# First norm's sums taken from a token-major copy of x on ScalarE; the low halves of w_in kept in DRAM after the first block

## Chip, core and metric

One core of a Trainium2 chip runs the whole layer in one launch. The metric is device time in microseconds (us) of that core. Five engines each work through their own list of instructions in order: PE (TensorE), DVE (VectorE), ACT (ScalarE), POOL (GpSimd) and SP (SyncE), which here issues every DMA. An instruction that must wait holds up all that stands behind it on its engine.

## The reference, cut to what matters

The layer works on 2048 tokens of 1024 channels in float32. What the change touches is the first norm and the first projection:

```
def rms_norm(x, g):
    ms = jnp.mean(x * x, axis=-1, keepdims=True)
    return x * lax.rsqrt(ms + EPS) * g

h = rms_norm(x, norm1_g)        # (2048, 1024)
proj = h @ w_in                 # (1024, 1536): 512 columns u, 512 xr, 512 yr
s5_out  = s5_mixer(proj[:, :512], ...)            # diagonal state space scan, GELU, GLU
lru_out = rglru_mixer(proj[:, 512:1024], proj[:, 1024:], ...)  # conv(4), gates, scan
mix = concat(rms_norm(s5_out), rms_norm(lru_out))
x = x + mix @ w_out
x = x + (silu(h2 @ w_gate) * (h2 @ w_up)) @ w_down,  h2 = rms_norm(x, norm2_g)
return rms_norm(x, final_g)
```

## The kernel before, in words

**Layout.** x lies in DRAM transposed (`xT`: channels by tokens), so a tile is 128 channels by 512 tokens. The 2048 tokens form four blocks of 512. Each float32 product is made of three matmuls in a faster float format: an operand a is split into a high half (`hi`, the value cast to that format) and a low half (`lo`, the value minus `hi`), and a·b is taken as hi·hi + hi·lo + lo·hi (`mm3`, L198).

**Input projection, `in_tb(b, t0)`, once for each block.** It splits x into `actH` and `actL` (L276 on ACT, L277 on DVE) and then runs 12 units, one for each 128 columns of `w_in`. A unit has two weight tiles ("parts") of 128x512, so a block has 24 parts. Class `Unit` loads a part (`wraw`, six buffers, L181), casts it on ACT (`whi`, four buffers, L187) and subtracts (`wlo`, four buffers, L188): on DVE for two units of three, on POOL for the third. The same parts of `w_in` are loaded and split again in each of the four blocks. The results are scaled by the norm's factor `rs` when they leave PSUM: `conv` (L627), `evac_u` (L618) and `gate_y` (L682), all on DVE. The first four units go through `conv` and `gates`, then come the gated recurrence (`decay`, `scan`) and `lru_out`.

**The norm's factor.** `SumSq` squares the eight channel tiles of a block on ACT (L238) and adds them up tile by tile on POOL (L240). In block 0 half of the squares are on POOL (L236) and the adds on DVE. `finish` sums over partitions with four small matmuls (L246), takes the reciprocal root in some twelve small DVE instructions (`rsqrt`, L210 to L218, tile `nv`), and spreads the result over partitions with four more matmuls (L256) and an ACT copy into `rs` (L259). In blocks 1 to 3 the tiles are loaded a second time for it, well ahead, through one buffer (`xq`, L272): a load waits until ACT has squared the tile before it.

**The S5 branch** runs beside the blocks. `s5_build` computes its tables on DVE, starting after the first `rsqrt`; POOL and PE help, and the tables go to DRAM (`md`). Its eight slices for the first half of the tokens (`s5_in`, `s5_scan`, `s5_out`) run during blocks 2 and 3 and end in `zb`, which the stage after the projection reads. After the four blocks come GLU and output projection (`glu_tb`, `out_tb`), then the feed-forward network with its weights split in the same way (L995, L996, matmuls L1156 and L1296).

**What sets the order.** The code files each step under a planned time (`at(t, fn)`) and emits the steps in order of these times; a scheduler with a timeline model of its own then sets the order of each engine's list. All DMAs stand in SP's one list. A DMA that writes a tile waits there until the tile's last reader is done, and each DMA also waits for the one eight before it.

Of the kernel before, what the change touches and what calls it, by code (L numbers as in the profile page):

```python
# [9 lines left out]
F32 = mybir.dt.float32  # L10
# [12 lines left out]
CT = 8  # L23
# [56 lines left out]
def build(tc, nc, I, O, ctx):  # L80
# [49 lines left out]
    td = dram("td", (2, 7, NSL, 128, TB))  # L130
    rld = dram("rld", (NB, TB))
# [36 lines left out]
    class Unit:  # L168


        def __init__(self, t, src, nk, eng=None):
            eng = DV if eng is None else eng
            self.parts = []
            for i in range(0, nk, 4):
# [8 lines left out]
                def split(part=part, n=n):  # L183
                    raw = part.pop("raw")[:, :n, :]
                    hi = part["hi"] = P.tile([128, 4, 128], R, tag="whi", name="whi", bufs=4)
                    lo = part["lo"] = P.tile([128, 4, 128], R, tag="wlo", name="wlo", bufs=4)
                    AC.copy(hi[:, :n, :], raw)  # L187
                    eng.tensor_tensor(out=lo[:, :n, :], in0=raw, in1=hi[:, :n, :].bitcast(F32), op=ALU.subtract)  # L188

                at(t + i * PT - 18.0, load)  # L190
                at(t + i * PT - 6.0, split)
# [30 lines left out]
    class SumSq:  # L222


        def __init__(self, n, tag="sum", bufs=1, room=(), dv=False):
            self.n, self.i, self.s, self.tag, self.bufs, self.room, self.dv = n, 0, None, tag, bufs, room, dv

        def add(self, ap):
            i, n = self.i, self.n
            self.i += 1  # L230
            if i == 0:
                q = self.s = A.tile([128, TB], F32, tag=self.tag, name=self.tag, bufs=self.bufs)
            else:
                q = self.room[i - 1] if i <= len(self.room) else t2("sq")
            if self.room and i % 2 == 0:
                GP.tensor_tensor(out=q, in0=ap, in1=ap, op=ALU.mult)  # L236
            else:
                AC.activation(out=q, in_=ap, func=AF.Square)  # L238
            if i:
                (DV if self.room or self.dv else GP).tensor_tensor(out=self.s, in0=self.s, in1=q, op=ALU.add)  # L240

        def finish(self, dst=None):
# [4 lines left out]
            y = rsqrt(ps[:, 0:4], 128 * self.n)  # L247
            ps = aux("nm")
# [344 lines left out]
    def in_tb(b, t0):  # L593
        H, L = actH, actL
        cur = {}
        room = [t[:, i, :] for t in xrp for i in range(2)] if b == 0 else ()
        ss, sl = SumSq(8, room=room), SumSq(4, "sumg", 2)
        tx, dx = (t0 - 6.5, 0.5) if b == 0 else (t0 - 5.0, 0.6)
        for k in range(8):
# [10 lines left out]
            if b == 0:  # L610
                at(tx + k * dx + 1.5, lambda k=k: ss.add(cur["x", k]))
            else:
                at(t0 - 62 + 1.5 * k, lambda k=k: ss.add(load_chunk(xT, b, k, pL, "xq", 1)))
        at(t0 + 0.1 if b == 0 else t0 - 48, lambda: cur.__setitem__("rs", ss.finish()))
# [884 lines left out]
```

## Time and profile before

| | us |
|---|---|
| median of 3 runs (lowest, highest) | 2208.16 (2206.6, 2210.63) |
| the profiled execution | 2207.93 |
| its span, first to last instruction | 2206.2 |
| four input blocks | 0 to 495 |
| GLU and output projection | 495 to 825 |
| feed-forward | 825 to 2206 |

The bounds of the stages are read from PE's rows of L198 and L1156: the first matmul of a block's 288 stands at 7, 122, 252 and 374 us, the last one of block 3 ends at 495. The page's times are in us from the first instruction. A group's row gives the line, the engine, the operation, output and inputs by the program's names, how often, and behind the bar the busy time, the mean in ns, and the idle time of the engine just before with what ended it. A row of a stretch (0.00:122.00) gives its length and, for each engine, the busy time and the number of instructions, then the granted PE clock as a share of full speed, the share of time in which the 16 DMA engines were busy, and GB/s.

### The profile page before, as it was taken

To read this page: it belongs to the slowest core of one execution; us is meant where nothing else is said; L and a number is where in the kernel's file an instruction comes from. 1 tells how busy PE (TensorE), PEld (TensorE's weight loads), DVE (VectorE), ACT (ScalarE), POOL (GpSimd) and SP (SyncE) were. 2 spreads that over 40 slices of the span, in tenths; PEclk is the share of its full clock that TensorE was granted. 3 is DMA by queue.
4 is the path that set the end of the run, shared out by engine and by line. 5 is a ranking of instruction groups with operands and counts; after the bars stand their busy time and mean duration, and the time that the engine had idled before them with its cause. 6 is when DMAs were issued, how large, how long until landed. Compare 5 with 4: busy or idle time off the path is not lost.

```text
span 2206.2 us, 26290 instructions
## 1 busy us (share of the span) xinstructions
PE 1988.3 (90%) x8632; PEld 1582.2 (72%) x8632; DVE 1335.3 (61%) x1975; ACT 812.1 (37%) x1336; POOL 1114.2 (51%) x904
## 2 busy tenths in 40 slices
PE   7668888878988978799999989999999999999996
PEld 5546666656766856577777767777777788888885
DVE  9998868759957397444444474444444535554744
ACT  4433644364344333223233253233232333333331
POOL 3768556649755377654554561231322326644442
PEclk9868999989898988899999999999999999999998
DMA  6244795573763687744444474443443568854733
GB/s 203 86 130 135 196 224 163 180 174 122 234 203 110 206 276 243 257 154 151 149 155 142 151 254 138 134 148 125 145 137 125 171 214 316 301 163 144 247 101 100
DMA packets 251754, 386.37 MB, mean 175 GB/s; under 512 B 59328, under 2 KB 81120, under 8 KB 251616
## 3 DMA queue, kind: packets, MB, share of 16 engines
q1 hardware_dynamic: 251616, 384.69, 55.5%
q8 instruction: 68, 1.11, 0.2%
q14 instruction: 70, 0.57, 0.1%
HBM read 267.92 MB, written 116.67 MB: 174 GB/s over the span
## 4 chain that ended last, share of the span: by engine, by line
PE 63%; DVE 16%; DMA 8%; POOL 5%; issue 4%; ACT 2%; SPq 1%; POOLq 0%; DVEq 0%; ACTq 0%
PE acc L1156 9%; PE gt L1156 9%; PE y L1156 9%; PE acc L198 6%; PE y L1296 5%; PE v L1156 5%; PE acc L1296 5%; PE gt L1296 5%; PE nm L1156 4%; PE nm L1296 2%; PE v L1296 2%; DVE wlo L188 2%; POOL s_s L824 2%; DMA xq<-xT 2%; DVE xh L633 1%
## 5 line engine op out<-in xcount | busy, mean ns | idle before, releaser
L1169 POOL TENSOR_TENSOR t<-t 128x512 f32<-128x512 f32 x66 | 100.6, 1525 | 343.8 <-DVE t L1195 242.2
L198 PE MATMUL acc<-actH,whi 128*128 128x512 f32 x528 | 219.5, 418 | 55.6 <-DVE gy L682 14.0
L995 ACT CAST whi<-ws 128x512 fp32r<-128x512 f32 x176 | 109.1, 620 | 343.1 <-PE gt L1156 91.8
L198 PE MATMUL acc<-actL,whi 128*128 128x512 f32 x528 | 219.7, 417 | 12.9 <-DVE actL L277 12.9
L198 PE MATMUL acc<-actH,wlo 128*128 128x512 f32 x528 | 217.5, 412 | 0.0
L996 DVE TENSOR_TENSOR wlo<-ws,whi 128x512 fp32r<-128x512 f32 x176 | 145.1, 825 | 67.3 <-ACT whi L995 65.3
L996 DVE TENSOR_TENSOR wlo<-ht,whi 128x512 fp32r<-128x512 f32 x112 | 106.0, 949 | 120.6 <-ACT whi L995 120.5
L198 PEld LDWEIGHTS acc<-actH,whi 128*128 128x128 f32 x528 | 105.7, 200 | 87.2 <-issue 35.1
L995 ACT CAST whi<-ht 128x512 fp32r<-128x512 f32 x154 | 95.0, 618 | 168.9 <-PE nm L1296 73.4
L1156 PE MATMUL y<-xh,whi 128*128 128x512 f32 x308 | 124.8, 405 | 16.9 <-ACT t L1188 12.0
L187 ACT CAST whi<-wraw 128x512 fp32r<-128x512 f32 x176 | 106.1, 613 | 86.5 <-PE acc L198 66.2
L996 POOL TENSOR_TENSOR wlo<-ht,whi 128x512 fp32r<-128x512 f32 x42 | 56.7, 1349 | 160.4 <-ACT whi L995 160.3
L198 PEld LDWEIGHTS acc<-actL,whi 128*128 128x128 f32 x528 | 105.6, 200 | 40.9 <-DVE actL L277 19.3
L1156 PE MATMUL acc<-xh,wlo 128*128 128x512 f32 x308 | 124.0, 403 | 8.4 <-DVE wlo L996 8.4
L1156 PE MATMUL acc<-xh,whi 128*128 128x512 f32 x308 | 124.6, 404 | 4.3 <-ACT xh L995 2.3
L1156 PE MATMUL y<-xh,wlo 128*128 128x512 f32 x308 | 123.4, 401 | 5.1 <-DVE wlo L996 5.1
L1156 PE MATMUL y<-xl,whi 128*128 128x512 f32 x308 | 123.9, 402 | 3.7 <-DVE xl L996 3.7
L188 POOL TENSOR_TENSOR wlo<-wraw,whi 128x512 fp32r<-128x512 f32 x64 | 93.9, 1470 | 64.2 <-ACT whi L187 63.7
L188 DVE TENSOR_TENSOR wlo<-wraw,whi 128x512 fp32r<-128x512 f32 x112 | 101.9, 914 | 39.1 <-ACT whi L187 32.3
L1156 PE MATMUL acc<-xl,whi 128*128 128x512 f32 x308 | 123.7, 402 | 1.4 <-DVE xl L996 1.4
L198 PEld LDWEIGHTS acc<-actH,wlo 128*128 128x128 f32 x528 | 106.3, 201 | 23.3 <-issue 0.9
L1156 PE MATMUL gt<-xh,whi 128*128 128x512 f32 x308 | 122.2, 397 | 0.5 <-DVE t L1193 0.5
(421 smaller groups left out, 5522.0 us busy)
## 6 DMA issues: line engine op xcount, KB each, us to landing
td<-t SPq DMA_DIRECT2D x154, 256.0 KB, 2.2
ht<-td SPq DMA_DIRECT2D x154, 256.0 KB, 2.8
wraw<-w_down SPq DMA_DIRECT2D x99, 256.0 KB, 4.5
wraw<-w_in SPq DMA_DIRECT2D x96, 256.0 KB, 3.9
scd<-ws SPq DMA_DIRECT2D x88, 256.0 KB, 2.2
ws<-scd SPq DMA_DIRECT2D x88, 256.0 KB, 2.6
wraw<-w_out SPq DMA_DIRECT2D x64, 256.0 KB, 3.5
xc<-xT SPq DMA_DIRECT2D x56, 256.0 KB, 4.3
```

The lines of the kernel that those rows point to most:

```text
L187: AC.copy(hi[:, :n, :], raw)
L188: eng.tensor_tensor(out=lo[:, :n, :], in0=raw, in1=hi[:, :n, :].bitcast(F32), op=ALU.subtract)
L198: PE.matmul(ps, lhsT=part[w][:, kw % 4, :], rhs=r_(x(kx)), start=first and i == 0 and j == 0, stop=last and i == n - 1 and j == 2)
L633: DV.scalar_tensor_tensor(out=xh[:, i, :], in0=xr[:, 1 + k:1 + k + TB], scalar=pc("cw", 4 * k + m), in1=xh[:, i, :], op0=ALU.mult, op1=ALU ...
L824: GP.tensor_tensor(out=sv[64 * ri:64 * ri + 64, gl, :, 1:], in0=a[p], in1=c[p], op=op)
L995: AC.copy(hi, raw)
L996: eng.tensor_tensor(out=lo, in0=raw, in1=hi.bitcast(F32), op=ALU.subtract)
L1156: PE.matmul(ps, lhsT=a[:, k, :], rhs=x, start=j in FIRST and k == 0 and i == 0, stop=k == 3 and i == 2, skip_group_check=True)
L1169: (DV if q == 0 else GP).tensor_tensor(out=g, in0=c, in1=g, op=ALU.mult)
L1296: PE.matmul(BK[p][i], lhsT=a[:, i, :], rhs=x, start=j in FIRST and s == 0 and v == 0, stop=s == NSL - 1 and v == 2, skip_group_check=True)
```

## The change

1. **Sums.** A second input `xn` holds x token by token (in the order of the blocks). For each block four tiles of 128 tokens by 1024 channels are loaded into the one `xq` buffer, now twice as large (512 KB a load), and one ACT instruction squares a tile and adds up along its row (`accum_out`). The four columns of sums go straight into `rsqrt`; `spread` is the second half of the old `finish`. The eight squares, the seven adds and the four summing matmuls of each block are gone. Block 0, which used the tiles of x that it had anyway, now loads its own four.
2. **Low halves.** In block 0 each `wlo` tile is also stored to DRAM (`wlc`, 24 stores of 256 KB). In blocks 1 to 3 a part's `lo` is loaded from there (72 loads of 256 KB) in place of the subtraction; the load of `wraw` and the cast to `whi` stay. `wlo` has five buffers in place of four, in all stages.

```diff
@@ class Unit
+        def __init__(self, t, src, nk, eng=None, keep=None, kept=None):
...
                     AC.copy(hi[:, :n, :], raw)
                     eng.tensor_tensor(out=lo[:, :n, :], in0=raw, in1=hi[:, :n, :].bitcast(F32), op=ALU.subtract)
+                    if keep is not None:
+                        SP.dma_start(keep[:, i:i + n, :], lo[:, :n, :].bitcast(F32))
+
+                def load_lo(part=part, i=i, n=n):
+                    lo = part["lo"] = P.tile([128, 4, 128], R, tag="wlo", name="wlo", bufs=5)
+                    SP.dma_start(lo[:, :n, :].bitcast(F32), kept[:, i:i + n, :])
+
+                def split_hi(part=part, n=n):
+                    raw = part.pop("raw")[:, :n, :]
+                    hi = part["hi"] = P.tile([128, 4, 128], R, tag="whi", name="whi", bufs=4)
+                    AC.copy(hi[:, :n, :], raw)

                 at(t + i * PT - 18.0, load)
+                if kept is not None:
+                    at(t + i * PT - 9.0, load_lo)
+                    at(t + i * PT - 6.0, split_hi)
+                    continue
                 at(t + i * PT - 6.0, split)
@@ in_tb
-        room = [t[:, i, :] for t in xrp for i in range(2)] if b == 0 else ()
-        ss, sl = SumSq(8, room=room), SumSq(4, "sumg", 2)
+        sl = SumSq(4, "sumg", 2)
+        ts = t0 - 4.0 if b == 0 else t0 - 58.0
...
-            if b == 0:
-                at(tx + k * dx + 1.5, lambda k=k: ss.add(cur["x", k]))
-            else:
-                at(t0 - 62 + 1.5 * k, lambda k=k: ss.add(load_chunk(xT, b, k, pL, "xq", 1)))
-        at(t0 + 0.1 if b == 0 else t0 - 48, lambda: cur.__setitem__("rs", ss.finish()))
+        def stat_load(i):
+            cur["q", i] = lt("xq", (128, DM), bufs=1)
+            SP.dma_start(cur["q", i], I["xn"][b * TB + 128 * i:b * TB + 128 * i + 128, :])
+
+        def stat(i):
+            if i == 0:
+                cur["ss"] = P.tile([128, 4], F32, tag="ssq", name="ssq", bufs=2)
+            q = cur.pop(("q", i))
+            AC.activation(out=q, in_=q, func=AF.Square, accum_out=cur["ss"][:, i:i + 1])
+
+        for i in range(4):
+            at(ts + 2.5 * i - (9.0 if b == 0 else 5.0), lambda i=i: stat_load(i))
+            at(ts + 2.5 * i, lambda i=i: stat(i))
+        at(ts + 9.0, lambda: cur.__setitem__("rs", SumSq.spread(rsqrt(cur["ss"], DM))))
...
-            u = Unit(t, I["w_in"][m], 8, GP if i % 3 == 2 else DV)
+            u = Unit(t, I["w_in"][m], 8, GP if i % 3 == 2 else DV, *((wlc[m], None) if b == 0 else (None, wlc[m])))
```

Three places of the built order. First, ACT in block 0 before, around the copy that makes `rs` (numbers behind a name tell tiles apart; `xq_288` to `xq_304` are tiles of block 1, `em` is a step of `s5_build`):

```order
L187 CAST whi_669<-wraw_334 128x512
L238 ACTIVATE sq_297<-xq_295 128x512
L259 COPY rs_224<-nm_219 128x512
L238 ACTIVATE sq_306<-xq_304 128x512
L187 CAST whi_712<-wraw_411 128x512
L149 ACTIVATE em_462<-p_466 128x256
L630 ACTIVATE xh2_101<-xr0_99,par_61 128x512
```

and the same stretch now, where `xq_127` and `xq_142` are the third and fourth tile of block 0 and `xq_221`, `xq_282`, `xq_293` the first three of block 1:

```order
L188 CAST whi_638<-wraw_320 128x512
L637 ACTIVATE xq_127,ssq_152<-xq_127 128x1024
L188 CAST whi_682<-wraw_391 128x512
L637 ACTIVATE xq_142,ssq_152<-xq_142 128x1024
L637 ACTIVATE xq_221,ssq_291<-xq_221 128x1024
L276 COPY rs_241<-nm_236 128x512
L637 ACTIVATE xq_282,ssq_291<-xq_282 128x1024
L658 ACTIVATE xh2_102<-xr0_100,par_61 128x512
L658 ACTIVATE xh2_102<-xr1_101,par_61 128x512
L637 ACTIVATE xq_293,ssq_291<-xq_293 128x1024
L188 CAST whi_737<-wraw_559 128x512
L150 ACTIVATE em_435<-p_439 128x256
```

The squares of block 1 still stand between the steps of block 0, but the copy to `rs` and the step `em` now have one and three larger tiles of block 1 ahead of them.

Second, SP in block 0 now, around the load of block 0's fourth tile (`wlo_639` and `wlo_683` are the eleventh and twelfth part, which POOL subtracts):

```order
L191 DMA wlc_90<-wlo_639 128x512
L182 DMA wraw_726<-w_in 128x512
L631 DMA xq_142<-xn 128x1024
L191 DMA wlc_90<-wlo_683 128x512
L182 DMA wraw_752<-w_in 128x512
L631 DMA xq_221<-xn 128x1024
L631 DMA xq_282<-xn 128x1024
L631 DMA xq_293<-xn 128x1024
L631 DMA xq_384<-xn 128x1024
L191 DMA wlc_90<-wlo_738 128x512
```

The fourth tile's load stands behind the store of the eleventh part's low half; fourteen of the sixteen loads of `xn` stand before the first load of a low half, and the last two among the first of these.

Third, DVE at block 1's first convolution, before:

```order
L627 TENSOR_TENSOR xr_99<-acc,rs 128x512
L627 TENSOR_TENSOR xr_100<-acc,rs 128x512
L188 TENSOR_TENSOR wlo<-wraw,whi 128x512 x2
L629 COPY halo<-xr_99 128x4
L629 COPY halo<-xr_100 128x4
L633 SCALAR_TENSOR_TENSOR xh_101<-xr_99,par,xh_101 128x512
L633 SCALAR_TENSOR_TENSOR xh_101<-xr_100,par,xh_101 128x512
L633 SCALAR_TENSOR_TENSOR xh_101<-xr_99,par,xh_101 128x512
L633 SCALAR_TENSOR_TENSOR xh_101<-xr_100,par,xh_101 128x512
L188 TENSOR_TENSOR wlo<-wraw,whi 128x512
```

and now:

```order
L655 TENSOR_TENSOR xr_101<-acc,rs 128x512
L657 COPY halo<-xr_100 128x4
L657 COPY halo<-xr_101 128x4
L661 SCALAR_TENSOR_TENSOR xh_102<-xr_100,par,xh_102 128x512
L661 SCALAR_TENSOR_TENSOR xh_102<-xr_101,par,xh_102 128x512
L661 SCALAR_TENSOR_TENSOR xh_102<-xr_100,par,xh_102 128x512
L661 SCALAR_TENSOR_TENSOR xh_102<-xr_101,par,xh_102 128x512
```

The subtractions between the steps of the convolution are gone; the rest of the list stands in nearly the same order, and the interleaving of S5 slices with PE's units is much the same in both.

More of the change, by code (lines that the diff above doesn't have):

```diff
@@ L130, in build @@
     td = dram("td", (2, 7, NSL, 128, TB))
+    wlc = dram("wlc", (12, 128, 8, 128))
     rld = dram("rld", (NB, TB))
@@ L168, in build @@
     class Unit:
-        def __init__(self, t, src, nk, eng=None):
+        def __init__(self, t, src, nk, eng=None, keep=None, kept=None):
             eng = DV if eng is None else eng
@@ L222, in build, with __init__ @@
     class SumSq:
-        def __init__(self, n, tag="sum", bufs=1, room=(), dv=False):
-            self.n, self.i, self.s, self.tag, self.bufs, self.room, self.dv = n, 0, None, tag, bufs, room, dv
+        def __init__(self, n, tag="sum", bufs=1, dv=False):
+            self.n, self.i, self.s, self.tag, self.bufs, self.dv = n, 0, None, tag, bufs, dv
         def add(self, ap):
@@ L233, in add @@
             else:
-                q = self.room[i - 1] if i <= len(self.room) else t2("sq")
-            if self.room and i % 2 == 0:
-                GP.tensor_tensor(out=q, in0=ap, in1=ap, op=ALU.mult)
-            else:
-                AC.activation(out=q, in_=ap, func=AF.Square)
+                q = t2("sq")
+            AC.activation(out=q, in_=ap, func=AF.Square)
             if i:
-                (DV if self.room or self.dv else GP).tensor_tensor(out=self.s, in0=self.s, in1=q, op=ALU.add)
+                (DV if self.dv else GP).tensor_tensor(out=self.s, in0=self.s, in1=q, op=ALU.add)
         def finish(self, dst=None):
@@ L247, in finish, with spread @@
             y = rsqrt(ps[:, 0:4], 128 * self.n)
+            return self.spread(y, dst)
+        @staticmethod
+        def spread(y, dst=None):
             ps = aux("nm")
@@ L1000, in wsplit @@
         hi = P.tile([128, 4, 128], R, tag="whi", name="whi", bufs=4)
-        lo = P.tile([128, 4, 128], R, tag="wlo", name="wlo", bufs=4)
+        lo = P.tile([128, 4, 128], R, tag="wlo", name="wlo", bufs=5)
         return split_w(raw, eng, hi, lo)
@@ L1467, in layout @@
     return {
+        "xn": np.ascontiguousarray(np.asarray(x)[0].reshape(NB, CB, CT, DM).transpose(0, 2, 1, 3)).reshape(SEQ, DM),
         "xT": np.ascontiguousarray(np.asarray(x)[0].reshape(NB, CB, CT, DM).transpose(3, 0, 2, 1)).reshape(DM, SEQ),
```

5 lines of the change are left out of this document (2 added, 3 removed).

## The prediction

> **What bounds the kernel now.** I read the stretches first: busy time of each engine in the four input blocks, the GLU and output stage and the feed-forward.
>
> ```profile
> 0.00:122.00 122.00, 88.14 (x344) 68.31 (x344) 116.69 (x284) 51.53 (x81) 65.15 (x77) 0.92 0.41 131
> 122.00:252.00 130.00, 97.07 (x423) 74.35 (x423) 118.57 (x128) 63.85 (x94) 94.33 (x63) 0.83 0.55 158
> 252.00:374.00 122.00, 103.13 (x510) 81.20 (x510) 96.65 (x155) 55.92 (x88) 70.37 (x68) 0.90 0.73 191
> 374.00:495.00 121.00, 96.82 (x460) 77.62 (x459) 85.70 (x142) 60.42 (x89) 69.70 (x80) 0.90 0.72 185
> 825.00:2206.20 1381.20, 1314.04 (x5595) 1051.91 (x5595) 677.61 (x908) 445.47 (x754) 599.42 (x411) 0.98 0.53 175
> ```
>
> The third number pair is DVE. It is busy 117 of 122 us in block 0 and 119 of 130 in block 1, then 97 and 86: DVE sets the pace of the first two blocks and shares it in the others. In the feed-forward PE is busy 1314 of 1381 us, and nothing there is touched but a buffer count, so I take no gain from it. A block has 312 matmuls of 512 columns (12 units x 8 x 3, and 24 of the gates); the chain of waits runs twelve such in 2.79 us.
>
> ```profile
> 951.48 2.79 PE gt L1156 x12
> ```
>
> So 312 matmuls are 73 us, and each block takes about 50 us more than that. Who holds PE up in block 1:
>
> ```profile
> PE acc L198 <- DVE actL L277: 10.5, 4, 3.8
> PE acc L198 <- DVE xr L627: 7.9, 3, 6.7
> PE acc L198 <- DVE h L675: 5.0, 1, 5.0
> PE acc L198 <- DVE y L682: 3.7, 1, 3.7
> PE acc L198 <- DVE us L618: 3.6, 1, 3.6
> ```
>
> These rows give us in total, times and the longest. All five are DVE: 30.7 us.
>
> **The change part by part.** First the low halves in block 1 (122 to 252 us).
>
> ```profile
> L188 DVE TENSOR_TENSOR wlo<-wraw,whi 128x512 fp32r<-128x512 f32 x18 | 21.3, 1189 | 4.9 <-ACT whi L187 2.6 <-ACT ig L149 2.3
> L188 POOL TENSOR_TENSOR wlo<-wraw,whi 128x512 fp32r<-128x512 f32 x8 | 13.3, 1659 | 27.6 <-ACT whi L187 27.5
> L240 POOL TENSOR_TENSOR sum<-sum,sq 128x512 f32<-128x512 f32 x7 | 12.1, 1735 | 0.2
> L188 DVE TENSOR_TENSOR wlo<-wraw,whi x18: 676/1026/2131, 121.9 to 251.7; 128x512 fp32r<-128x512 f32 x18
> L633 DVE SCALAR_TENSOR_TENSOR xh<-xr,par,xh 128x512 f32<-128x512 f32 x12 | 15.2, 1297 | 0.0
> ```
>
> Of a block's 24 parts DVE subtracts 16: 16 x 1.189 = 19.0 us leave DVE. POOL loses 13.3 + 12.1 = 25.4 of its 94.3 us. That is worth something to DVE too, since a DVE instruction that starts under a POOL one is stretched:
>
> ```profile
> 34.48 0.17 DVE L308 TENSOR_SCALAR xq<-xf 128x16 f32<-128x16 f32 x1
> 34.53 1.35 POOL L240 TENSOR_TENSOR sum<-sum,sq 128x512 f32<-128x512 f32 x1 [11.01 <-DVE cr L379]
> 34.64 1.28 DVE L381 TENSOR_TENSOR cr<-cr,ci 128x16 f32<-128x16 f32 x1
> ```
>
> The same size takes 0.17 us free and 1.28 under a POOL add. The whole overrun is not in one row; the subtractions show 1189 against a least of 676 ns, 0.51 us each, and the convolution's L633 has a mean of 1297. If the remaining DVE work of block 1 (118.6 - 19.0 = 99.6) overruns in the share of the subtractions (0.51/1.19 = 0.43), that is 43 us, and POOL's cut by 25.4/94.3 = 0.27 returns up to 11; nothing if POOL's remaining work moves into the gaps. So DVE needs 19 to 30 us less. The whole of it can't pass, since PE's waits on DVE were 30.7 and the two PSUM tiles of `acc` still hand over at DVE: I take -20, bounds 0 and -30.
>
> The Trainium skill, "SBUF — State Buffer", section "Who interferes with whom", has the shared port pair of DVE and GpSimd as an exclusive lock held for the whole instruction. By that rule each of the 15 POOL instructions gone could free DVE for its full length, 25 us in place of my 0 to 11, and the sum would come out about 15 us lower; the 1.28 us row agrees with the lock, but no row says how many of the 15 met a waiting DVE.
>
> Block 2 (252 to 374).
>
> ```profile
> L188 DVE TENSOR_TENSOR wlo<-wraw,whi 128x512 fp32r<-128x512 f32 x18 | 17.6, 978 | 12.1 <-ACT whi L187 7.7 <-issue 4.3
> L238 ACT ACTIVATE sq<-xq 128x512 f32<-128x512 f32 x7 | 4.4, 629 | 22.2 <-DMA xq<-xT 22.2
> 305.87 6.89 DMA xq<-xT
> ```
>
> 16 x 0.978 = 15.6 us leave a DVE that is busy 97 of 122, so most is slack. ACT stands 22.2 us before the squares of the next block's tiles, and one such load (6.89 us) is on the chain of waits at 306; by the built order all of these loads now stand at the latest among the first steps of block 1. I take -10: that chain piece and a fifth of the DVE work. Bounds 0 (all slack) and -24 (both in full, rounded).
>
> Block 3 (374 to 495).
>
> ```profile
> L188 DVE TENSOR_TENSOR wlo<-wraw,whi 128x512 fp32r<-128x512 f32 x15 | 11.6, 787 | 1.0 <-ACT whi L187 1.0
> SPq L758 <- DVE s_ta L817: 15.7, 4, 5.5
> ```
>
> 11.6 us of DVE, which idles 35 of 121 here. I take -4, bounds +4 and -12.
>
> **What the new DMAs cost.** A tile of 256 KB goes out and comes back in the feed-forward like this:
>
> ```profile
> scd<-ws SPq DMA_DIRECT2D x88, 256.0 KB, 2.2
> ws<-scd SPq DMA_DIRECT2D x88, 256.0 KB, 2.6
> hx<-x1d SPq DMA_DIRECT2D x16, 512.0 KB, 5.0
> mi<-md SPq DMA_DIRECT2D x16, 512.0 KB, 4.5
> ```
>
> A stored tile lands in 2.2 us, a reload in 2.6 and up. With five `wlo` buffers, four parts (4 x 2.79 = 11 us of PE) lie ahead of the one in use, so a reload of even 6 us is hidden if SP issues it at once. SP does not always: in block 3 it stood 15.7 us for the S5 buffers, at most 5.5 at a time, and the reloads now queue behind such waits, as do the loads of `wraw` as before. 5.5 + 5 is just under 11, so I cost it at nothing, and up to 10 us a block if the cover goes (a rival below). The stores of block 0 wait for the subtraction that frees the same `wraw` tile, which the next load waited for anyway: nothing. The engines' time: block 2 has 0.73 x 122 = 89 us of DMA for 191 GB/s x 122 us = 23.3 MB; 24 reloads are 6.3 MB, at that rate 24 us. 89 + 24 = 113 us fits a block of 122 - 10 = 112 only just, block 3 with 0.72 x 121 = 87 + 24 = 111 likewise; that is why I take no more there.
>
> **Block 0** is where the change can lose. Its seven adds leave DVE and four squares POOL, but the sums now need four loads through one buffer, with ACT waiting in line.
>
> ```profile
> L240 DVE TENSOR_TENSOR sum<-sum,xr x4: 678/680/1522, 9.5 to 17.6; 128x512 f32<-128x512 f32 x4
> 29.93 0.33 SPq L272 DMA_DIRECT2D xq<-xT  x1
> 34.48 0.33 SPq L272 DMA_DIRECT2D xq<-xT  x1
> 35.85 1.32 POOL L188 TENSOR_TENSOR wlo<-wraw,whi 128x512 fp32r<-128x512 f32 x1
> 38.43 0.57 ACT L259 COPY rs<-nm 128x512 f32<-128x512 f32 x1
> 43.27 0.41 ACT L149 ACTIVATE em<-p 128x256 f32<-128x256 f32 x1
> 45.53 0.28 DVE L338 TENSOR_SCALAR p<-em 128x256 f32<-128x256 f32 x1
> 46.90 1.29 POOL L240 TENSOR_TENSOR sum<-sum,sq 128x512 f32<-128x512 f32 x1 [1.31 <-ACT sq L238]
> 59.25 1.29 POOL L240 TENSOR_TENSOR sum<-sum,sq 128x512 f32<-128x512 f32 x1 [3.06 <-ACT sq L238]
> L149 ACT ACTIVATE T<-T 128x1024 f32<-128x1024 f32 x4 | 4.2, 1049 | 0.0
> ```
>
> One round (issue 0.33, landing 4.5 to 5.0, an ACT pass over 1024 columns 1.05) is about 6 us, against 4.5 between the two old loads. The fourth load stands on SP behind the store of the eleventh part, which POOL finished at 37.2 before; without the adds ahead of it, say 36.5. Its square ends at 42.5; the next square, block 1's first, stands ahead of the copy to `rs` and ends at 48.5. So `rs` is there at 49 in place of 39, and after two more rounds `em` at 61.5 in place of 43.7. DVE meets `em` (L338) at 45.5 now, later by 16. Part of this is filled: the built order has six convolution steps, one subtraction and one evacuation moved ahead of it, about 8 x 0.75 = 6 us. And of the POOL adds of block 1's sums four came after this point (the two L240 rows are the first and the last); each may have stretched a DVE instruction by the 1.1 us seen above: 4 us. 16 - 6 - 4 = +6, bounds 0 (rounds as short as the old 4.5, all filled) and +12 (no relief from POOL). What is late next is the table build behind `em`, and with it S5.
>
> The Trainium skill, "DMA: Bandwidth & Descriptors", section "Anatomy of one DMA — SWDGE (gpsimd) path", fits a DMA at 2.0 us plus its bytes over 436 GB/s, which is 3.2 us for 512 KB (an estimate from that page, made for another issuing engine than this). A round would be 4.6 us, the three rounds 4 us shorter and block 0's term about +2. The rows of this trace, 4.5 and 5.0, disagree, and I go by them.
>
> **The sum.** +6 - 20 - 10 - 4 = -28 against the profiled 2207.9 (its span 2206.2 and 1.7 around it; the median of the three runs is 2208.2): 2180 us. ACT's own load hardly moves: 28 squares of 0.63 us before, 16 of 1.05 now.
>
> **Rivals.**
>
> 1. *Only block 1 gains.* S5's in-order turns (SP's 15.7 us, 25 us of DVE idle) keep blocks 2 and 3 where they are. For it: DVE's idle time there. Against: the 22.2 us that ACT stood. +6 - 20 gives 2194.
> 2. *DMA takes the place of DVE.* Reloads arrive late, PE waits for `wlo` in blocks 2 and 3, +5 each on their old times (half of the 10 above). For it: 113 and 111 us of DMA work, DMA share 0.73. Against: the five buffers. +6 - 20 + 10 gives 2204.
> 3. *Slower: the late tables carry through.* The ACT queue in block 0 delays `em` by 18 us and the tables with it; if S5's slices set the end of block 3, blocks 1 to 3 finish no earlier and block 0's +12 stays: 2220. It decides once S5's first half ends later than PE's last units.
>
> ```profile
> 440.58 3.51 DMA zb<-u
> 444.59 3.71 DMA zA<-zb
> ```
>
> Against: the first half's last store is at 441, 54 us before block 3's end, more than the delay.
> 4. *More than forecast.* Bounds of blocks 1 to 3 near their far ends (-28, -20, -8) with block 0 at +2 give 2154.
>
> That the change does not do what it says is little likely, since the built order has the subtractions gone.
>
> **How the numbers follow.** Chances: forecast 0.48 (its own range 2165 to 2193), only block 1 0.17, DMA 0.12, slower 0.15, more 0.08. Runs of this kernel tell about 0.2%, 4.4 us, from no change. Faster: 0.48 + 0.17 + 0.08 and a little of the DMA case, 0.02 = 0.75 (that case mostly lands within 4.4 us of the start, 0.06, or above it, 0.04). Same 0.06 and 0.01 of rival 3: 0.07. Slower 0.18. The range runs from 2142, the sum of the far bounds (0 - 30 - 24 - 12 = -66), to 2221, which takes in rival 3's 2220.
>
> **What would show it.** Right: DVE's busy time in block 1's stretch under 100 us, PE's waits on DVE there cut by two thirds, no ACT wait on `xq` past the first 20 us of block 1, block 0 ending near 128. Wrong: PE waiting for `wlo` by DMA (rival 2), the S5 rows of zb at 441 or later while PE waits on S5 (rival 3), block 0 ending after 134 or before 118, or block 1 still at 125 us or more with DVE idle.

## The result

The changed kernel takes 2173.41 us (median; 2166.04 to 2180.55) against 2207.38 us for the kernel before beside it: a ratio of 0.9845, 95% interval 0.9809 to 0.9882, or 34.0 us less. The forecast was 28 us less, so sign and size came out. The sum did so with two wrong terms that nearly cancel: block 1 gained 10 us in place of 20, block 2 gained 21 in place of 10, and about 7 of these 21 are S5 work that moved into block 3.

Stage lengths in us, in the profiled execution of each kernel, between the same matmuls in all of them (first of each block's 288, last of block 3, last of the output projection). In the kernel before the output projection ends at 809 us, and the feed-forward's first matmul stands there too; the 825 of the table ahead is 16 us late. The column "slices" counts the S5 slices (the first step of each on PE) that run within block 2. The rows below the second are the experiments. A stage length is of one execution, and executions of one kernel lie up to 15 us apart in total, so a difference of a few us in one stage tells little by itself.

| kernel | block 0 | 1 | 2 | slices | 3 | GLU, out | feed-forward | median | ratio to before (95%) |
|---|---|---|---|---|---|---|---|---|---|
| before | 115.1 | 129.7 | 122.3 | 6 | 121.1 | 313.8 | 1397.1 | 2207.4 | 1 |
| the change | 117.7 | 119.7 | 101.3 | 5 | 114.6 | 317.4 | 1395.3 | 2173.4 | 0.9845 (0.9809, 0.9882) |
| sums alone | 118.5 | 128.9 | 120.0 | 8 | 108.4 | 314.4 | 1380.9 | 2181.8 | 0.9890 (0.9867, 0.9912) |
| reload alone | 115.7 | 121.2 | 95.0 | 3 | 141.6 | 311.7 | 1394.4 | 2189.9 | 0.9923 (0.9899, 0.9947) |
| old sums in block 0 | 105.8 | 122.5 | 103.8 | 6 | 123.0 | 308.1 | 1391.7 | 2163.5 | 0.9807 (0.9780, 0.9834) |
| before, five `wlo` buffers | 116.5 | 130.1 | 122.1 | 6 | 120.7 | 311.9 | 1393.6 | 2204.0 | 0.9985 (0.9970, 0.9999) |
| reload of DVE's parts only | 120.5 | 121.0 | 94.6 | 5 | 119.2 | 318.0 | 1390.7 | 2174.9 | 0.9862 (0.9836, 0.9887) |
| reload of POOL's parts only | 116.0 | 131.4 | 114.6 | 8 | 106.0 | 313.8 | 1376.7 | 2168.2 | 0.9843 (0.9809, 0.9877) |
| sums in blocks 1 to 3 only | 109.9 | 127.5 | 107.8 | 6 | 122.0 | 312.0 | 1382.2 | 2171.0 | 0.9848 (0.9819, 0.9876) |
| the change, S5 slices late | 117.7 | 120.1 | 87.6 | 3 | 140.3 | 309.6 | 1389.6 | 2178.0 | 0.9878 (0.9847, 0.9908) |
| old sums in block 0, DVE's parts only | 108.0 | 129.9 | 106.0 | 5 | 116.2 | 318.9 | 1384.7 | 2173.9 | 0.9859 (0.9843, 0.9875) |
| old sums in block 0, no reload in block 3 | 107.8 | 124.0 | 104.8 | 6 | 126.6 | 320.6 | 1382.9 | 2172.1 | 0.9849 (0.9824, 0.9873) |
| the change, buffers for tiles 0 and 2 | 110.1 | 116.5 | 114.0 | 8 | 106.5 | 312.1 | 1380.2 | 2148.8 | 0.9743 (0.9723, 0.9762) |
| the change, buffers for tiles 1 and 2 | 104.7 | 120.9 | 95.6 | 5 | 117.3 | 318.2 | 1400.4 | 2165.7 | 0.9842 (0.9802, 0.9881) |

### The profile page after: what moved, and what is told of

Read it like the earlier page. It is cut to its first block, busy times and chain, and to the rows that moved or that the text cites. A ratio compares the mean times of both kernels' runs of the same rounds, so it can differ in the third digit from the quotient of the medians.

```text
span 2173.4 us, 26158 instructions
## 1 busy us (share of the span) xinstructions
PE 1956.8 (90%) x8600; PEld 1564.3 (72%) x8600; DVE 1244.8 (57%) x1920; ACT 815.4 (38%) x1340; POOL 1042.6 (48%) x855
## 4 chain that ended last, share of the span: by engine, by line
PE 55%; DVE 4%; DMA 4%; POOL 3%; issue 2%; ACT 1%; SPq 0%; POOLq 0%; DVEq 0%; ACTq 0%
PE gt L1184 9%; PE acc L1184 9%; PE y L1184 9%; PE v L1184 5%; PE nm L1184 5%; PE y L1324 4%; PE acc L1324 4%; PE gt L1324 4%; PE v L1324 2%; PE nm L1324 2%; PE acc L214 2%; DVE wlo L1024 1%; DMA ht<-xcd 1%; DVE hx L1059 1%; DMA wraw<-w_down 1%
## 5 line engine op out<-in xcount | busy, mean ns | idle before, releaser
L1024 DVE TENSOR_TENSOR wlo<-ht,whi 128x512 fp32r<-128x512 f32 x112 | 107.1, 957 | 126.3 <-ACT whi L1023 122.1
L1024 DVE TENSOR_TENSOR wlo<-ws,whi 128x512 fp32r<-128x512 f32 x176 | 134.1, 762 | 33.7 <-ACT whi L1023 33.6
L1024 DVE TENSOR_TENSOR wlo<-wraw,whi 128x512 fp32r<-128x512 f32 x88 | 72.0, 818 | 142.2 <-ACT whi L1023 142.2
L1184 PE MATMUL acc<-xh,wlo 128*128 128x512 f32 x308 | 122.3, 397 | 9.6 <-DVE wlo L1024 9.6
L1184 PE MATMUL gt<-xh,wlo 128*128 128x512 f32 x308 | 121.3, 394 | 0.0
L1184 PE MATMUL gt<-xl,whi 128*128 128x512 f32 x308 | 121.2, 394 | 0.0
```

The source lines that it names most:

```text
L1024: eng.tensor_tensor(out=lo, in0=raw, in1=hi.bitcast(F32), op=ALU.subtract)
L1184: PE.matmul(ps, lhsT=a[:, k, :], rhs=x, start=j in FIRST and k == 0 and i == 0, stop=k == 3 and i == 2, skip_group_check=True)
```

## The profile after

The stretches of the four blocks and of the feed-forward, with the columns as before (PE, PEld, DVE, ACT, POOL busy, then granted clock, DMA share, GB/s):

```profile
0.00:125.10 125.10, 82.71 (x328) 65.48 (x329) 100.58 (x273) 63.96 (x102) 51.10 (x65) 0.88 0.71 239
125.10:244.80 119.70, 94.00 (x418) 71.50 (x419) 93.41 (x119) 57.90 (x86) 67.79 (x49) 0.84 0.68 203
244.80:346.10 101.30, 91.05 (x467) 73.12 (x466) 63.25 (x126) 52.66 (x80) 39.23 (x46) 0.95 0.92 255
346.10:460.80 114.70, 95.95 (x483) 75.75 (x482) 76.65 (x130) 60.01 (x87) 57.06 (x76) 0.94 0.90 246
778.10:2173.40 1395.30, 1315.83 (x5619) 1056.24 (x5617) 681.05 (x921) 450.24 (x762) 621.37 (x418) 0.98 0.53 176
```

DVE lost 16 us of busy time in block 0 (116.7 to 100.6), 25 in block 1, 33 in block 2 and 9 in block 3. In blocks 1 to 3 PE is now the busiest of the five engines (in block 1 by 0.6 us only), and the DMA engines are at 0.92 and 0.90 in blocks 2 and 3, where the prediction saw room only just.

**Block 0.** Waits of DVE and PE in it (total, times, longest), then, from two views and in order of time, SP's issues of the second, third and fourth load of `xn` and the ACT rows around them:

```profile
DVE nv L226 <- ACT xq L637: 11.2, 1, 11.2
DVE wlo L189 <- DMA wlc<-wlo: 3.3, 1, 3.3
PE nm L273 <- DVE nv L234: 13.9, 2, 11.7
```

```profile
17.27 0.40 SPq L631 DMA_DIRECT2D xq<-xn  x1
24.12 1.06 ACT L637 ACTIVATE xq<-xq 128x1024 f32<-128x1024 f32 x1 [1.57 <-DMA xq<-xn]
26.11 0.33 SPq L631 DMA_DIRECT2D xq<-xn  x1
31.85 1.06 ACT L637 ACTIVATE xq<-xq 128x1024 f32<-128x1024 f32 x1 [0.61 <-DMA xq<-xn]
34.86 0.33 SPq L631 DMA_DIRECT2D xq<-xn  x1
40.66 1.06 ACT L637 ACTIVATE xq<-xq 128x1024 f32<-128x1024 f32 x1 [5.82 <-DMA xq<-xn]
41.63 0.19 ACT L637 ACTIVATION_READ_ACCUMULATOR xq<-xq 128x1 f32 x1
45.14 1.06 ACT L637 ACTIVATE xq<-xq 128x1024 f32<-128x1024 f32 x1 [3.32 <-DMA xq<-xn]
46.36 0.59 ACT L276 COPY rs<-nm 128x512 f32<-128x512 f32 x1
55.71 0.41 ACT L150 ACTIVATE em<-p 128x256 f32<-128x256 f32 x1
```

The fourth square ends at 41.7, one square of block 1 goes ahead of `rs`, and `rs` is there at 46.4. DVE stood 11.2 us for that square and PE 11.7 us behind DVE. Block 0's own squares begin 7.7 and 8.8 us apart (24.12, 31.85, 40.66): each load lands 5.7 to 6.9 us after its issue, by the start of the square that waited for it. The DMA engines are full in that time, at a share of 0.59 before and 1.05 now (the same stretch of the kernel before, then of the change):

```profile
17.00:35.00 18.00, 18.00 (x79) 14.88 (x78) 16.50 (x65) 6.06 (x11) 2.08 (x3) 1.00 0.59 202
```

```profile
17.00:35.00 18.00, 15.54 (x69) 12.55 (x67) 6.83 (x16) 7.27 (x12) 2.87 (x4) 1.00 1.05 398
```

From the fourth square on, with the DMA engines at 0.32 from 41 to 55 us, a round of load and square is 4.4 to 4.6 us (40.66, 45.14, 49.75, 54.14). The stores weren't free: DVE waits for one (`wlc`), and with the sums alone, where there are none, the share in that stretch is 0.89 and the fourth square begins 5.8 us sooner, at 34.84.

**Block 1.** It falls into two halves. The first 43 us before and after (one fence for each kernel), then the rest:

```profile
122.00:165.00 43.00, 25.72 (x68) 18.53 (x69) 43.00 (x41) 18.76 (x26) 28.46 (x16) 0.64 0.53 163
165.00:252.00 87.00, 71.35 (x357) 55.82 (x355) 75.57 (x88) 45.09 (x68) 65.87 (x48) 0.92 0.56 155
```

```profile
125.00:168.00 43.00, 23.85 (x59) 15.94 (x60) 42.97 (x40) 16.75 (x25) 27.94 (x15) 0.67 0.59 181
168.00:245.00 77.00, 70.35 (x361) 55.72 (x360) 50.74 (x81) 41.44 (x61) 39.85 (x34) 0.93 0.73 215
```

In the first 43 us DVE is never idle, before or after, and PE does 68 matmuls before, 59 now. The six subtractions that DVE did in this half before are gone:

```profile
L188 DVE TENSOR_TENSOR wlo<-wraw,whi 128x512 fp32r<-128x512 f32 x6 | 5.9, 989 | 0.0
```

DVE now runs S5 table steps in their room, ahead of and between the splits of x that PE needs (the rows from 126 us on, in order of time):

```profile
126.36 0.68 DVE L527 TENSOR_TENSOR tab<-tab,kk 128x512 f32<-128x512 f32 x1
126.97 0.68 DVE L529 TENSOR_TENSOR tab<-tab,se 128x512 f32<-128x512 f32 x1
127.57 0.68 DVE L528 TENSOR_TENSOR tmp<-tab,se 128x512 f32<-128x512 f32 x1
128.17 0.68 DVE L530 TENSOR_TENSOR tmp<-tab,kk 128x512 f32<-128x512 f32 x1
128.77 1.21 DVE L698 TENSOR_TENSOR T<-T,xh 128x1024 f32<-128x1024 f32 x1
129.91 1.40 DVE L294 SCALAR_TENSOR_TENSOR actL<-xc,par,actH 128x512 fp32r<-128x512 f32 x2
```

So PE's wait for those splits grew from 10.5 us to this:

```profile
PE acc L214 <- DVE actL L294: 16.1, 4, 7.0
PE acc L214 <- DVE y L710: 6.1, 1, 6.1
```

All of block 1's gain is in the second half, 87 to 77 us, and there it is used up: PE is busy 70.4 of 77.

**Block 2.** PE's waits, the largest first, and the new transfers of the whole kernel (KB each, median us from issue to landing where the landing is known; of block 0's four loads of `xn` only the first is):

```profile
PE acc L214 <- DMA wlo<-wlc: 6.9, 1, 6.9
PE acc L214 <- ACT actH L293: 2.1, 1, 2.1
```

```profile
wlo<-wlc SPq DMA_DIRECT2D x72, 256.0 KB, 4.4
xq<-xn SPq DMA_DIRECT2D x16, 512.0 KB, 3.5
wlc<-wlo SPq DMA_DIRECT2D x24, 256.0 KB, 5.6
```

Once a reload came 6.9 us late: the second rival's mechanism, at two thirds of the price that it had for a block, in one place. Gone are two waits of PE for the small steps of the norms (`nv`), 8.5 us in the kernel before:

```profile
PE nm L250 <- DVE nv L218: 4.7, 1, 4.7
PE nm L256 <- DVE nv L218: 3.8, 1, 3.8
```

S5's tables weren't late in the end. Their last stores to DRAM stand at 284.3 before and 265.2 now, S5's first matmul at 301.7 and 288.3 (rows: ns least, median, most; first and last start). Before:

```profile
L483 SPq DMA_DIRECT2D md<-ti x8: 320/366/424, 206.9 to 284.3; - x8
L773 PE MATMUL v<-u,mi x256: 272/273/477, 301.7 to 598.0; 128*64 128x128 f32 x128
```

and now:

```profile
L500 SPq DMA_DIRECT2D md<-ti x8: 319/354/602, 196.0 to 265.2; - x8
L801 PE MATMUL v<-u,mi x256: 272/273/421, 288.3 to 569.0; 128*64 128x128 f32 x128
```

## The experiments

The first theory was the prediction's own. It fell back step by step to the one that stands at the end of this section.

**Each part alone.** The change without the reload and with four buffers:

```diff
-            u = Unit(t, ..., GP if i % 3 == 2 else DV, *((wlc[m], None) if b == 0 else (None, wlc[m])))
+            u = Unit(t, ..., GP if i % 3 == 2 else DV)
```

> The first part of the change alone: sums from the token-major copy, every block still subtracts its own low halves (four wlo buffers). Theory (the sums lose in block 0, where ACT and DVE wait for xn, and win in block 2, where ACT no longer waits for xq): block 0 +6, block 1 -2 (seven POOL adds fewer), block 2 -9, block 3 0, so about -5 us against the kernel before. Rival (the sums carry the gain, by freeing ACT and SP in blocks 1 and 2): -20 or more. Second rival (block 0's loss is all that they do): +3 to +6.

and the kernel before with the reload and five buffers:

```diff
-            u = Unit(t, ..., GP if i % 3 == 2 else DV)
+            u = Unit(t, ..., GP if i % 3 == 2 else DV, *((wlc[m], None) if b == 0 else (None, wlc[m])))
-    ... tag="wlo", name="wlo", bufs=4)
+    ... tag="wlo", name="wlo", bufs=5)
```

> The second part alone: low halves stored by block 0 and reloaded in blocks 1 to 3, five wlo buffers, old sums. Theory (DVE and POOL time freed in blocks 1 to 3 is the gain, and block 0 has no loss): block 0 0 to +2, block 1 -12, block 2 -12, block 3 -5, about -28 us. Rival (the low halves give little without the sums, because ACT still waits for xq in block 2): -12 us. If the two parts add up, this and the sums alone give -34 together.

The sums alone gave 26 us where the theory had 5, so it fell; but 16 us of it are in the feed-forward, which the sums don't touch, and up to its start they gave 12. The reload alone gave 18, between the theory's 28 and the rival's 12: 27 in block 2 and 8.5 in block 1, with 20 given back in block 3, where three more of the S5 slices stand. Up to the start of the feed-forward the two parts give 12 and 17 alone, the change 31: so far they add up.

**The old sums in block 0.** The change, with block 0's sums from its own tiles on ACT, POOL and DVE as before:

```diff
-        for i in range(4):
-            at(ts + 2.5 * i - (9.0 if b == 0 else 5.0), lambda i=i: stat_load(i))
+        if b == 0:
+            at(t0 + 0.1, lambda: cur.__setitem__("rs", ss0.finish()))
+        else:
+            ...
```

> The whole change, but block 0 sums its squares in the old way from the x tiles it has; blocks 1 to 3 use the token-major copy. Theory (block 0 loses 6 us by waiting for its four xn loads, and nothing else depends on it): block 0 ends near 118 instead of 125, total 6 to 8 us below the changed kernel, about 2166. Rival (block 0's end is set by the table build on DVE and by the stores of the low halves, so the wait is only moved): within 3 us of the changed kernel.

2163.5 us, 10 us under the change where 6 to 8 were expected; block 0 fell by 11.9 us to 105.8, and DVE's wait for the fourth square isn't there.

**The buffer count alone.** The kernel before with `wlo` in five buffers:

```diff
-    ... tag="wlo", name="wlo", bufs=4)
+    ... tag="wlo", name="wlo", bufs=5)
```

> The kernel before with five wlo buffers instead of four and nothing else. Theory (the fifth buffer is there to hold reloads and gives nothing by itself): within 4 us of the kernel before. Rival (the fifth buffer lets DVE and POOL subtract further ahead and is a part of the gain, in the feed-forward too): -8 us or more. It also shows how far a change that only makes the scheduler choose again moves the time.

2204.0 against 2207.7 beside it, as expected: the fifth buffer is worth 4 us at most.

**Whose subtractions.** The reload for DVE's parts only, and for POOL's only:

```diff
-*((wlc[m], None) if b == 0 else (None, wlc[m])))
+*(() if i % 3 == 2 else (wlc[m], None) if b == 0 else (None, wlc[m])))    # the other: i % 3 != 2
```

> The change with only the 16 parts of DVE's units stored and loaded again; POOL goes on subtracting its 8 parts in every block (13 us of POOL a block, by the kernel before's 1.659 us each). If the gain of the reload is that DVE has 16 subtractions less, most of it stays: blocks 1 and 2 within 4 us of the change's 119.7 and 101.3, total 2165 to 2183. PE's one wait of 6.9 us for wlo by DMA should be gone or under 3 us, since a third of the reloads is gone. If the gain is POOL's (fewer POOL instructions that stretch DVE's), blocks 1 and 2 lose 6 to 10 us each against the change and the total is 2188 or more.

> The change with only the 8 parts of POOL's units stored and loaded again; DVE goes on subtracting its 16 parts in every block (about 19 us of DVE in block 1, 16 in block 2). If the gain of the reload is DVE's, block 2 goes back towards the 120 us that it takes with the sums alone (115 or more), block 1 towards 128, and the total is near the 2182 of the sums alone. If it is POOL's, block 2 stays near 103. In this build seven of the eight S5 slices of the first half stand ahead of block 3 in PE's list and the last at its first matmul (the change: five ahead), so block 3 and the GLU and output stage together should take about 425 us in place of 432.

DVE's parts alone leave blocks 1 and 2 at 121.0 and 94.6, the second even under the change, and the total within 2 us of it. POOL's alone put them back to 131.4 and 114.6. In block 1 no S5 slice runs in any of these kernels, so there the comparison is clean. Block 2 isn't comparable: it holds eight slices with POOL's parts alone, five in the change. With eight slices it takes 120.0 us without a reload (the sums alone), 114.6 with POOL's parts, and 114.0 with all parts (the version with buffers for tiles 0 and 2 below). These are the last two, POOL's parts first:

```profile
254.60:369.30 114.70, 102.46 (x555) 81.27 (x555) 92.52 (x181) 51.54 (x80) 58.48 (x71) 0.95 0.76 215
```

```profile
234.30:348.30 114.00, 100.84 (x560) 80.05 (x558) 82.48 (x165) 55.96 (x88) 57.96 (x72) 0.97 0.92 269
```

DVE is busy 10 us less in the second, and the block is no shorter. With a third of the reloads gone PE's wait for them in block 2 is less than half as long:

```profile
PE acc L214 <- DMA wlo<-wlc: 3.0, 1, 3.0
```

So in block 1 the reload's gain is DVE's 16 subtractions, as the prediction had it (131.4 to 119.7); in block 2, by these two runs, they are worth next to nothing. The total of the second is 2168.2 all the same, not 2182: block 3 with the next stage took 420 us and the feed-forward 1376.7, the least of all (below).

**The sums in blocks 1 to 3 alone.** Old sums in block 0, no reload, four buffers. Against the run with the old sums in block 0:

```diff
-            u = Unit(t, ..., GP if i % 3 == 2 else DV, *((wlc[m], None) if b == 0 else (None, wlc[m])))
+            u = Unit(t, ..., GP if i % 3 == 2 else DV)
-    ... tag="wlo", name="wlo", bufs=5)
+    ... tag="wlo", name="wlo", bufs=4)
```

> The token-major sums in blocks 1 to 3 only; block 0 takes its sums from its own tiles as in the kernel before, and nothing is reloaded (four wlo buffers). If block 0's own loads of xn are what costs there, block 0 takes 105 to 108 us (118.5 with the sums in all blocks, 105.8 with the reload and old sums in block 0). Theory that the sums in blocks 1 to 3 bring S5 forward: S5's first matmul on u at 270 to 280 us (kernel before 302), six of eight slices ahead of block 3, block 3 with the GLU and output stage 425 to 433 us; total 2170 to 2190, lower by 16 only if the feed-forward begins in the order that the run with the sums alone had. Rival, that the parts simply add: the change with the old sums in block 0 (2163) less the gain of the reload alone (18) gives 2181 as well, but with S5's first matmul where the kernel before has it.

Block 0 took 109.9 us, 2 above the expectation, and S5's first matmul stands at 278.7, as expected; the total of 2171.0 is at the low end of its range, with a feed-forward of 1382. Block 2, with six slices as in the kernel before, took 107.8 in place of 122.3, and 103.8 with the reload too (old sums in block 0). With this run the parts can be set against each other. From the first matmul to the end of the output projection (the first five columns of the table added) the kernel before takes 802 us, the reload alone 785, these sums alone 779, both 763: 17 and 23 less, and 39 less together. Block 0's own loads then cost 11 us without the reload (779 to 790) and 8 with it (763 to 771).

The run also shows what POOL's work does to DVE. In block 0 it has the kernel before's own sums, only block 1's squares and adds are off POOL; before and here:

```profile
0.00:122.10 122.10, 88.14 (x344) 68.31 (x345) 116.79 (x284) 51.63 (x81) 65.15 (x77) 0.92 0.41 131
```

```profile
0.00:117.10 117.10, 83.80 (x336) 65.44 (x336) 110.67 (x284) 60.32 (x99) 57.19 (x70) 0.92 0.52 170
```

DVE has 284 instructions in both, 282 of them the same, and is busy 6.1 us less, with 8.0 us of POOL gone (seven adds). The Trainium skill, "SBUF — State Buffer", section "Who interferes with whom", has the port pair that DVE and GpSimd share as a lock held for a whole instruction; 6.1 of 8.0 us agrees with that better than the prediction's 0 to 11 of 25, though which instruction met which isn't seen.

**The place of S5's slices.** With the reload alone five of the eight S5 slices of the first half were left for block 3, in the change three (rows of S5's first matmuls in block 3, 16 a slice; the change, then the reload alone):

```profile
L801 PE MATMUL v<-u,mi 128*64 128x128 f32 x80 | 6.1, 301 | 2.7 <-DMA u<-ub 2.2 <-DMA mi<-md 0.2 <-PE y L863 0.2
```

```profile
L789 PE MATMUL v<-u,mi 128*64 128x128 f32 x112 | 9.2, 301 | 5.1 <-DVE s_tb L797 3.9 <-DMA mi<-md 1.2
```

(The stretch holds some of the second half too.) To see whether that is what makes block 3 long, the change was run with the first slice held behind the ninth unit of block 2:

```diff
-    ts0 = 130
+    ts0 = 184
+            with tc.issue_after(last["mm", 2, 8]):     # around s5_in(0, 0)
-    for g, (ts, dt) in enumerate(((ts0, 10), (tP1 - 10.0, 7))):
+    for g, (ts, dt) in enumerate(((ts0, 5), (tP1 - 10.0, 7))):
```

> The change with one thing moved: the first S5 slice of the first half is held behind the ninth unit of block 2 on PE (its planned time 184 in place of 130, the slices 5 apart), so that three slices stand ahead of block 3 and five in it, as in the run with the reload alone; the change has five and three. If the place of the slices is what makes block 3 long there (141.6 against 114.6), then here block 2 takes 94 to 98 us, block 3 135 to 145, block 3 with the GLU and output stage 448 to 455 (the change 432), and the total is 2184 to 2193. If block 3 is long there because the old sums stand in it, block 3 here stays within 5 us of 115 and the total within 5 of 2173.

Half of it came true. Block 3 went to 140.3, and with the next stage to 449.9, so the slices' place makes it long. But block 2 fell to 87.6, below the 94 to 98 expected, so that only 4.4 us were lost at the end of the output projection. Where a slice stands moves time between stages, some 7 us a slice here (block 2 from 101.3 with five to 87.6 with three), and hardly changes the sum.

**Two versions put together by adding.** Old sums in block 0 with DVE's parts only, and old sums in block 0 with the subtractions back in block 3:

```diff
+*(() if i % 3 == 2 else (wlc[m], None) if b == 0 else (None, wlc[m])))              # the first
+*((wlc[m], None) if b == 0 else () if b == 3 else (None, wlc[m])))                  # the second
```

> The run with the old sums in block 0 (2163), with only the 16 parts of DVE's units loaded again in blocks 1 to 3. The parts have added up so far (from the kernel before, input blocks with the GLU and output stage: reload alone -17, sums in blocks 1 to 3 alone -23, both -39), and the change with only DVE's units reloaded stood 2 us above the change there, so this stage should take 763 + 2 = 765 us. PE's list of the feed-forward is row for row the one of the run with POOL's units reloaded (1376.7 us); the change and four other runs share another list (1390 to 1395). If the list alone makes that difference, the feed-forward takes 1375 to 1379 here and the total is 2150 (2145 to 2155). If it was the earlier stages that made it, the feed-forward takes 1390 or more and the total is 2162 or more.

> The run with the old sums in block 0 (2163), with the lower parts subtracted in block 3 as in the kernel before; only blocks 1 and 2 load them again. Block 3 with the GLU and output stage took 431 to 435 us in all runs with two or three S5 slices left for block 3, with the reload and without. If the reload gains nothing in block 3, these two stages take 428 to 434 us here (431 with the reload in block 3). If it gains the 4 us of the prediction or more, they take 435 to 443. PE's list of the feed-forward is the one that took 1376.7; with that the total is 2149 (2144 to 2155) in the first case and 2157 or so in the second.

Both missed, by 24 and 23 us. The feed-forward was 6 to 8 us longer than forecast. Of the rest, most lies in the GLU and output stage, 318.9 and 320.6 against 308.1 in the run that they were made from, which neither edit touches; why wasn't settled. In the first, block 1 also took 129.9 in place of 122.5 (POOL busy 86.8 us there against 68.6 with the full reload), no less than with the sums in blocks 1 to 3 only (127.5): that DVE's subtractions are block 1's gain is shown for the change, and this kernel doesn't bear it out. In the second, block 3 took 126.6 in place of 123.0. What POOL's parts and block 3's reload are worth stays open, and the adding of parts holds for the four kernels above but missed by 14 and 21 us in these two.

**Block 0's loads through more buffers.** The change, with two of block 0's four tiles loaded into the two `xr` tiles, which are still free then, so that no two following loads wait for the one `xq`:

```diff
+            if b == 0 and i in (0, 2):       # the second version: (1, 2), and ts = t0 - 8.0
+                cur["q", i] = xrp[(0, 2).index(i)].rearrange("p a b -> p (a b)")[:, 0:DM]
+            else:
                 cur["q", i] = lt("xq", (128, DM), bufs=1)
```

> The whole change, but in block 0 the first and the third tile of xn go to the two xr buffers (the old sums used them as room in block 0), so that no load waits there for the square two tiles before it through the one xq buffer more than once. If the rounds through the one buffer are block 0's cost, DVE's wait of 11.2 us for the fourth square goes to under 4 us, rs is made at 39 us or before (46.4 in the change), block 0 takes 104 to 109 us (117.7), and the input blocks with the GLU and output stage together 761 to 766 us (770.7). If the loads' share of the DMA engines at the start is the cost (2 MB more among the first tiles of x and w_in), block 0 stays above 113. The feed-forward has the list of 1376.7 here too, so the total is 2147 in the first case and 2156 in the second; seven of the eight S5 slices stand ahead of block 3.

> The whole change with the second and the third xn tile of block 0 in the xr buffers, and block 0's four loads and squares planned 4 us earlier. Unlike the run with the first and third tile there (2148.8), PE's list of the feed-forward is the change's own here, and five S5 slices stand ahead of block 3 as in the change. So it tells what the buffers alone are worth: if it is the 8 us by which block 0 got shorter there, block 0 takes 105 to 111 us (117.7), the input blocks with the GLU and output stage 759 to 764 us (770.7), the feed-forward 1389 to 1395, and the total is 2159 to 2167. If most of the 24.6 us came from the other order of the later stages and the start of block 0 is paid back in block 1, the total stays at 2168 or more.

The first is the fastest of all kernels here: 2148.8 us, 0.9743 (0.9723 to 0.9762) of the kernel before and 24.6 us under the change. In block 0 DVE waits for the fourth square only this long, and `rs` is made at 34.1:

```profile
DVE nv L226 <- ACT xq L640: 1.1, 1, 1.1
```

Block 0 is 7.6 us shorter, not the 8.7 to 13.7 expected, while the stages up to the feed-forward sum to 759, better than the 761 to 766 expected; the total is near the 2147 expected. The second has the change's own order of the feed-forward, and shows what the buffers (and 4 us of earlier planned time) do without a gain there: block 0 104.7, 13 us less; 757 up to the feed-forward, 14 less; 2165.7, within its range although the feed-forward of 1400 is 5 us above its own. In the first the fourth load was issued at 21.75, 13 us sooner than in the change, and it still took 5.75 us to its square (27.50), with the DMA share from 17 to 35 us at 1.05 again. So the rounds through one buffer were block 0's cost, each of them long while the DMA engines were full. It is not paid back in block 1.

**The feed-forward.** Its length differs by up to 24 us over the kernels, though nothing in it was edited but the buffer count. The built orders sort them. PE's list there is, row for row, the same in the change and six others (reload alone, old sums in block 0, five buffers, DVE's parts only, late slices, tiles 1 and 2): 1390 to 1400 us. It is a second one in four (POOL's parts only, the two put together by adding, tiles 0 and 2): 1377 to 1385. The means of the two are 1394 and 1381. The other three kernels have lists of their own, with 1397 (before), 1381 and 1382 (sums alone, sums in blocks 1 to 3). The first hundred us of the change, then of POOL's parts only:

```profile
778.10:878.10 100.00, 65.72 (x243) 48.04 (x242) 69.35 (x76) 29.53 (x50) 72.34 (x46) 0.84 0.80 264
```

```profile
789.10:889.10 100.00, 78.11 (x294) 58.42 (x293) 76.12 (x82) 33.57 (x57) 74.70 (x47) 0.86 0.80 274
```

PE does 51 matmuls more in them, with the DMA share alike. PE's largest wait of the change there, on the weight split, isn't among the other's:

```profile
PE acc L1184 <- DVE wlo L1024: 9.6, 1, 9.6
```

That the order is the cause rests on this sorting alone; no run changed that order and nothing else. By the profiled executions the fastest kernel lies 26.4 us under the change: 15.1 of them here, 11.5 in the earlier stages.

**What stands:** the reload pays by DVE's subtractions in block 1 of the change (one other kernel doesn't bear this out), and by little in block 2 at the same number of S5 slices; the sums pay in blocks 1 to 3 (23 us, most of it in block 2) and cost 8 to 11 us in block 0 through the one buffer; where S5's slices fall only shifts time between stages; and the scheduler's order at the start of the feed-forward goes with some 13 us.

## Why the prediction was right, and where it wasn't

**Block 0: +2.6, forecast +6.** The mechanism held: four loads through one buffer, ACT in line, `rs` and `em` late. The round was put at 6 us throughout, and it was 7.7 and 8.8 for block 0's own tiles (loads of 5.7 to 6.9 us while the DMA engines were full) and 4.4 to 4.6 for block 1's behind them. The fit of the Trainium skill, "DMA: Bandwidth & Descriptors", section "Anatomy of one DMA — SWDGE (gpsimd) path", comes to an estimate of 3.2 us a load and 4.6 a round: the loads from 42 to 60 us agree with it (3.2 to 3.5 us), block 0's own don't. Since the rounds behind the fourth square were the short ones, `rs` was 8 us late, not 10 (46.4 against 38.4), `em` 12.4, not 18. The stall was put in the wrong place: DVE stood 11.2 us for the fourth square, ahead of `rs`, and none of the steps named filled that. What was set against it was too small: with block 1's old sums gone block 0 is 5 us shorter where it keeps its own (115.1 to 109.9), 9 with the reload besides, where 4 stood. Cost 9 to 12 less relief 5 to 9 gives the small plus, so that the term came out near is in part luck.

**The new DMAs: "nothing".** Wrong by small amounts. A store landed in 5.6 us, not 2.2, and DVE waited once, 3.3 us, for one; a reload landed in 4.4, and PE waited once, 6.9 us. Both prices were rows of the feed-forward, whose DMA share is 0.53; here it is 0.68 to 0.92. In block 0 the stores also stand among the loads of `xn`, whose fourth square is 5.8 us later than without them.

**Block 1: -10.0, forecast -20.** DVE's saving was right (25 us, within 19 to 30; busy 93.4, under the 100 that was named). The failing step is "I take -20": it let the saving pass as if it were spread over the block. In its first 43 us DVE stays full with S5 table steps and the recurrence, and PE's wait on the x splits grew by 5.6 us; in the rest PE came to 91% busy. "PE's waits on DVE cut by two thirds" is wrong for the same reason: for `acc` they went from 30.7 to 26 us. What the prediction called "late next", the table build, was named in block 0 and not priced in block 1. But with `em` back at 43.4 us (tiles 1 and 2) block 1 is still 120.9, and with `em` at 57.2 (tiles 0 and 2) it is 116.5, so the delay of `em` isn't what holds it there; the amount of table work on DVE is the remaining candidate, which no run tested.

**Block 2: -21.0, forecast -10.** About 7 of the 21 are a shift that the forecast didn't have: one S5 slice fewer runs in it (PE's S5 matmuls, the rows that read `mi` and `mo`, take 11.6 us in place of 18.5). Of the rest the failing step is the "chain piece" of 6.9 us, which stood for all that the sums do: with six slices each, the sums in blocks 1 to 3 take 14.5 us off the block (122.3 to 107.8), with PE's two waits for `nv`, 8.5 us, gone. In the change `rs` for block 3 is made at 270.5, before at 372.6. The reload takes 4 more (103.8), about the fifth of DVE's work that was booked (3.1). So DVE's slack did swallow most of that saving, although DVE's busy time fell by 33 us, not 15.6. PE's idle time went from 18.9 to 10.3 us (stretch less busy), its busy time from 103.1 to 91.1, with 44 matmuls fewer (32 of them the slice's) at a higher granted clock (0.90 to 0.95). Whether the waits went because the loads come earlier or because POOL's adds are gone, no run separates.

**Block 3: -6.5, forecast -4**, within its bounds, although it took over that slice. **GLU and output +3.6, feed-forward -1.8**, forecast 0; right for the change, by luck of the order as the other kernels show.

**Rivals.** Only block 1 gains: refuted, blocks 2 and 3 together gained 27.5 us (243.4 to 215.9), which a slice that moves from one to the other doesn't change. DMA takes DVE's place: refuted in its size, since PE waited for a reload once, 6.9 us, 3.0 with a third fewer reloads, and the blocks got shorter; but the DMA engines are at 0.92 in block 2. Late tables carry through: `em` was late, but the tables' last stores came 19 us earlier and S5 began 13 us earlier, so its condition was never met. More than forecast: the change isn't there; the version with buffers for tiles 0 and 2 is, at 2148.8.

## What to carry to other kernels

Before a saving on the busiest engine is booked, cut the stage into pieces: it passes only where that engine paces and up to the point where the next one is full, and work that was queued elsewhere may take its room. Before two kernels' times for a stage are compared, count what else runs in it: here S5 slices that moved between blocks looked like a gain. A row of loads through one buffer at the start of a program costs its rounds, the more so while the DMA engines are full, and a buffer that is not needed yet can be lent for them. Where a scheduler sets the order, compare stage by stage and look at the lists of stages that weren't edited: here two of them differed by 13 us, where the whole gain was 34.

## What the runs showed that was not expected

Each ACT square with `accum_out` is followed by an instruction of its own that reads the sums out, 15 in the first 125 us:

```profile
L637 ACT ACTIVATION_READ_ACCUMULATOR xq<-xq 128x1 f32 x15 | 2.8, 185 | 0.0
```

0.185 us each, beside the 1.06 of the square. The prediction's ACT sum left it out; ACT wasn't the bound, so it cost nothing to see.
